# Reading moving operands and writing products in woven runs, in four gate products of a ConvFFN

## The chip, the cores and the metric

The kernel runs on one core of a Trainium2 chip. The metric is the device time of one execution in microseconds (us). The engines are named as the profile names them: PE is TensorE (PEld its weight loads), ACT is ScalarE, DVE is VectorE, POOL is GpSimd, and SP issues the transfers from HBM.

## The reference

The program computes a small decoder trunk in fp32 on 256 tokens of width 2048: one mLSTM layer, a gated ConvFFN, one layer of differential attention, a second ConvFFN and a last norm. The change lies in the first ConvFFN:

```python
def conv_ffn(xn, w_up, conv_w, conv_b, w_down):
    u = xn @ w_up                                  # (256, 2048) @ (2048, 2 * 5632)
    up = jnp.pad(u, ((0, 0), (CONV_W - 1, 0), (0, 0)))
    c = conv_b + up[:, 0:S] * conv_w[0]
    for j in range(1, CONV_W):
        c = c + up[:, j:j + S] * conv_w[j]
    gate, val = jnp.split(c, 2, axis=-1)
    return (jax.nn.silu(gate) * val) @ w_down
```

## The kernel before

Every fp32 number is split into two parts of type fp32r, a rounded high part and the low part that is left, and a product of two numbers is the sum of three products of parts (the one of both low parts is left out). TensorE multiplies a stationary operand of 128 x 128 with a moving operand of up to 512 columns and adds into a PSUM accumulator.

The up projections are computed by `gemm`. One call makes one *column pair*, 256 columns of the projection, from 16 k tiles of 128. Weights are stationary: each column half of a k tile (128 columns) is loaded once as its high part `wh` and once as its low part `wl`. Activations are the moving operand. For each k tile the high part `xh` (256 tokens) and the low part `xl` (256 tokens) lie side by side in one buffer, `xhl`. So per k tile and column half there are two matmuls on L411: `wh` against `xhl`, 512 columns into the whole accumulator, and `wl` against `xh`, 256 columns into its lower half. When the 16 k tiles are done, ScalarE copies the upper half of each of the two accumulators out (`low`, L417), VectorE adds it to the lower half (L418), and the caller's function takes the sum on.

Weights arrive by DMA as `raw`, 1 MB at a time; `granule` splits them four k tiles at a time: ScalarE writes the high parts (L376) and VectorE the low parts (L377) into one of five buffers `w2`. A call of `gemm` thus has four granules, k0 = 0, 4, 8 and 12, of 16 matmuls each.

`conv_ffn` goes through the projection in two parts of 11 pairs. For pair j of a part it calls `gemm` for the gate columns and then `gemm` for the value columns. Behind a gate call stand the convolution and a SiLU on ScalarE (L871), behind a value call the convolution and the product of gate and value (L881). A scheduler sets the order of all engines from the order in which the program is written, with small tasks put off by a number of granules (`later`, `tick`).

Of the kernel before, what the change touches and what calls it, by code (L numbers as in the profile page):

```python
# [19 lines left out]
P = 128  # L20
# [23 lines left out]
X_AT = (1, 2, 3, 5, 6, 8, 9)  # L44
SQ_AT = (6, 8, 10, 12)
CW = 256
WCOLS = 2048


# [19 lines left out]
def trunk(  # L69
# [22 lines left out]
    def tmp(name, rows=P, dt=F32):  # L92
        return work.tile([rows, T], dt, tag="tmp", name=name, bufs=8)
# [20 lines left out]
    def later(granules, fn):  # L114
        clock[1] += 1
        heapq.heappush(waiting, (clock[0] + granules, clock[1], fn))

    def tick():
        clock[0] += 1
        while waiting and waiting[0][0] <= clock[0]:  # L120
            heapq.heappop(waiting)[2]()
# [176 lines left out]
    def split(value, name):  # L298
        h, l, hl = block(F32R, name)
        act.activation(h, value, AF.Copy)  # L300
        dve.tensor_tensor(l, value, h.bitcast(F32), op=ALU.subtract)
        return h, l, hl
# [57 lines left out]
    def granule(w, c0, cw, k0, kn, raws, j, own=True):  # L360

        kc, hc = WCOLS // cw, WCOLS // cw // 2
        at, hc = k0 % kc, min(hc, kn - k0)
        if at == 0:
            raws[j] = wpool.tile([P, kc, cw], F32, tag="raw", name="raw", bufs=RAW)
            n = min(kc, kn - k0)
            loads.append(nc.sync.dma_start(raws[j][:, :n], w[k0 * P:(k0 + n) * P, c0:c0 + cw].rearrange("(k p) n -> p k n", p=P)))
        part = raws[j][:, at:at + hc]
        if not own:
            pairs = [block(F32R, "w2")[:2] for _ in range(hc)]  # L370
            for i, (h, l) in enumerate(pairs):
                act.activation(h, part[:, i], AF.Copy)
                dve.tensor_tensor(l, part[:, i], h.bitcast(F32), op=ALU.subtract)
            return pairs
        w2 = wpool.tile([P, WCOLS // cw // 2, 2, cw], F32R, tag="w2", name="w2", bufs=HL)
        act.activation(w2[:, :hc, 0], part, AF.Copy)  # L376
        dve.tensor_tensor(w2[:, :hc, 1], part, w2[:, :hc, 0].bitcast(F32), op=ALU.subtract)  # L377
        return [(w2[:, i, 0], w2[:, i, 1]) for i in range(hc)]

    def in_order(kn, hc, groups, lead, held=1):  # L380

        starts, groups = list(range(0, kn, hc)), list(groups)
        order = [(j, k) for j in groups[:lead] for k in starts[:-held]] + [(j, k) for j in groups[:lead] for k in starts[-held:]]
        return order + [(j, k) for j in groups[lead:] for k in starts], starts[-1]

    def gemm(xs, w, col0, pairs, evac, lead=1, narrow=()):

        kn = len(xs)
        order, last = in_order(kn, 4, pairs, lead)
        raws, accs = {}, {}
        for j, k0 in order:
            if k0 == 0:
                accs[j] = [acc_ps.tile([P, 2 * T], F32, tag="acc", name="acc") for _ in range(2)]
            ps = accs[j]
            halves = granule(w, col0 + j * CW, CW, k0, kn, raws, j)
            wide = j not in narrow
            for i, (wh, wl) in enumerate(halves):  # L400
                k = k0 + i
                xh, xl, xhl = xs[k]
                for n in range(2):
                    s = slice(n * P, (n + 1) * P)
                    one = ps[n][:, :T]
                    if wide:
                        ops = ((wh[:, s], xhl, ps[n]), (wl[:, s], xh, one))
                    else:
                        ops = ((wh[:, s], xh, one), (wh[:, s], xl, one), (wl[:, s], xh, one))
                    for o, (a, b, to) in enumerate(ops):  # L410
                        pe.matmul(to, a, b, start=(k == 0 and o == 0), stop=(k == kn - 1 and o == len(ops) - 1))  # L411
            if k0 == last:
                done = accs.pop(j)
                if wide:
                    for p in done:
                        low = tmp("low")
                        act.activation(low, p[:, T:], AF.Copy)  # L417
                        dve.tensor_tensor(p[:, :T], p[:, :T], low, op=ALU.add)  # L418
                evac(j, [p[:, :T] for p in done])
            tick()  # L420

    def gemm_tokens(xs, w, col0, groups, evac, cw=G, lead=1):

        kn, hc = len(xs), WCOLS // cw // 2
        order, last = in_order(kn, hc, groups, lead, held=4 // hc)
# [82 lines left out]
    def gemm_by_tokens(xs, w, col0, evac):  # L508
# [3 lines left out]
        for t in range(2):  # L512
            s = slice(t * P, (t + 1) * P)
            for k in range(kn):
                if t == 0 and k % 4 == 0:

                    halves += granule(w, col0, CW, k, kn, raws, 0, own=k < HL * 4)
                xh, xl, _ = xs[k]
# [8 lines left out]
    def mix(pair):  # L527

        (a11, a21), (a12, a22) = ((c[:, :P], c[:, P:]) for c in pair)
        s = block(F32, "sum")[2].rearrange("p (a n) -> p a n", a=4)  # L530
        dve.tensor_tensor(s[:, 0], a21, a22, op=ALU.add)
        dve.tensor_tensor(s[:, 1], s[:, 0], a11, op=ALU.subtract)
        dve.tensor_tensor(s[:, 2], a21, a11, op=ALU.subtract)
        dve.tensor_tensor(s[:, 3], a12, s[:, 1], op=ALU.subtract)
        h, l = (block(F32R, "mix")[2].rearrange("p (a n) -> p a n", a=4) for _ in range(2))
        act.activation(h, s, AF.Copy)
        dve.tensor_tensor(l, s, h.bitcast(F32), op=ALU.subtract)
        return [(h[:, i], l[:, i]) for i in range(4)]
# [42 lines left out]
    def residual(norm):  # L581
        def evac(g, ps, mix=None):
            if mix is not None:
                mixed_in(g, mix)
            for t in range(2):
                rows = stream[:, t, g * G:(g + 1) * G]
                dve.tensor_tensor(rows, ps[t], rows, op=ALU.add)
            if norm is not None:
                norm.add(g)
        return evac  # L590
# [87 lines left out]
    def mlstm(norm):  # L678
# [5 lines left out]
        def gates():  # L684
            gw = wpool.tile([P, WCOLS], F32, tag="raw", name="gw", bufs=RAW)[:, :KD * 16].rearrange("p (k n) -> p k n", n=16)

# [163 lines left out]
    def conv_ffn(layer, norm, evac_down, finish=None):  # L850

        cw = convs[layer]
        later(2, norm.rstd)
        half = FT // 2
        for part in range(2):
            hidden = [None] * half
            conv_of = {}

            def conv(ps, f):
                u = tmp("u")  # L860
                dve.tensor_tensor(u, ps, norm.r, op=ALU.mult)  # L861
                c = tmp("c")
                act.activation(c, u, AF.Identity, bias=cw[:, 3, f:f + 1], scale=cw[:, 2, f:f + 1])  # L863
                dve.scalar_tensor_tensor(c[:, 1:], u[:, :T - 1], cw[:, 1, f:f + 1], c[:, 1:], op0=ALU.mult, op1=ALU.add)
                dve.scalar_tensor_tensor(c[:, 2:], u[:, :T - 2], cw[:, 0, f:f + 1], c[:, 2:], op0=ALU.mult, op1=ALU.add)
                return c

            def evac_gate(j, ps):
                for n in range(2):
                    c = conv(ps[n], part * half + 2 * j + n)  # L870
                    act.activation(c, c, AF.Silu)  # L871
                    conv_of[2 * j + n] = c

            mixed = {}

            def evac_val(j, ps):
                pair = []
                for n in range(2):
                    f = 2 * j + n
                    c = conv(ps[n], FT + part * half + f)  # L880
                    dve.tensor_tensor(c, c, conv_of[f], op=ALU.mult)  # L881
                    hidden[f] = split(c, f"hid{f}")
                    pair.append(c)
                if 4 * (j // 2) in MIXED:
                    mixed[2 * j] = mix(pair)

            for j in range(half // 2):
                gemm(norm.sets[0], w_up[layer], part * half * P, [j], evac_gate)
                gemm(norm.sets[0], w_up[layer], D_FF + part * half * P, [j], evac_val)
            rows = w_down[layer, part * half * P:(part + 1) * half * P]  # L890
            if part == 0:
                gemm_sevenths(hidden, mixed, rows, 0, range(NG), residual(None), MIXED)
            elif finish is None:
                gemm_sevenths(hidden, mixed, rows, 0, range(NG), evac_down, MIXED)
            else:
                gemm_sevenths(hidden, mixed, rows, 0, range(NG - 1), evac_down, MIXED)
                finish(hidden, rows)
# [239 lines left out]
    def finish(hidden, rows):  # L1137
        gemm_tokens(hidden, rows[:, W0:], 0, [0], lambda j, ps: evac_last(NG - 1, ps), cw=T)
        gemm_by_tokens(hidden, rows, W1, tokens_done)

    conv_ffn(1, norm_f1, evac_last, finish=finish)


# [29 lines left out]
```

## Time and profile before

| What | Value |
|---|---|
| Three runs | 2247.5, 2247.64, 2247.94 us; median 2247.64 us |
| Profiled execution, span from the first to the last instruction | 2246.0 us |
| Mean granted TensorE clock | 0.999 |
| PE busy in the span | 2236.4 us |
| DVE, ACT, POOL busy | 1800.5, 1297.7, 112.4 us |
| Bytes read from HBM, rate over the span | 414.77 MB, 186 GB/s |

The page gives the span of the profiled execution and no other time of it; the runs are timed apart from it. Busy time is the time in which an engine had an instruction under way. Matmuls overlap their neighbours: the mean duration that a row gives for one is longer than its share of TensorE's time, which is read from a stretch of many matmuls divided by their count. Shapes stand as partitions x elements.

### The profile page before, as it was taken

How to read it: one execution, taken by the hardware profiler on the slowest of the kernel's cores; microseconds unless marked ns; L12 is line 12 of the kernel's file. 1: busy time of each engine (PE TensorE's matmuls, PEld its weight loads, DVE VectorE, ACT ScalarE, POOL GpSimd, SP SyncE). 2: the span in 40 equal slices, each digit the busy share in tenths (PEclk: the TensorE clock that was granted, in tenths of full speed). 3: DMA queues.
4: the chain of work that ended last, by engine and by line, in shares of the span. 5: the costliest groups of instructions: out<-in, count | busy, mean ns of one | idle time of the engine just before them, and what ended most of it. 6: DMA issues, size and time to landing. Idle time of an engine off the chain costs nothing.

```text
span 2246.0 us, 33469 instructions
## 1 busy us (share of the span) xinstructions
PE 2236.4 (100%) x12847; PEld 1953.4 (87%) x12847; DVE 1800.5 (80%) x3007; ACT 1297.7 (58%) x2011; POOL 112.4 (5%) x275
## 2 busy tenths in 40 slices
PE   9999999999999999999999999999999999999998
PEld 9888888888888888888888888888888888888888
DVE  6756868787788877879998985677877988778896
ACT  5455655665554565656655655556565555556554
POOL 0014000000000000000022102300000000000000
PEclk9999999999999999999999999999999999999999
DMA  8554546555545755546566555465555457555464
GB/s 278 177 176 149 186 162 211 192 188 188 187 160 188 234 188 188 190 148 206 193 204 196 161 173 162 154 202 187 188 188 188 159 188 245 190 189 189 145 216 150
DMA packets 325636, 419.04 MB, mean 187 GB/s; under 512 B 9102, under 2 KB 238820, under 8 KB 325476
## 3 DMA queue, kind: packets, MB, share of 16 engines
q1 hardware_dynamic: 325444, 416.89, 56.7%
q8 instruction: 101, 1.65, 0.3%
q14 instruction: 59, 0.48, 0.1%
q10 hardware_dynamic: 32, 0.01, 0.0%
HBM read 414.77 MB, written 2.10 MB: 186 GB/s over the span
## 4 chain that ended last, share of the span: by engine, by line
PE 99%; DVE 0%; ACT 0%; issue 0%; DVEq 0%
PE acc L411 54%; PE acc L503 16%; PE acc L437 14%; PE mix L493 6%; PE acc L493 4%; PE acc L656 2%; PE val_ps L335 1%; PE acc L521 1%; PE turn_ps L231 0%; PE as_ps L987 0%; PE warm_ps L130 0%; PE turn_ps L637 0%; PE hn_ps L357 0%; PE gps L695 0%; PE as_ps L988 0%; PE an_ps L357 0%
## 5 line engine op out<-in xcount | busy, mean ns | idle before, releaser
L377 DVE TENSOR_TENSOR w<-raw,w 128x1024 fp32r<-128x1024 f32 x679 | 826.6, 1222 | 269.6 <-ACT w L376 267.3
L376 ACT ACTIVATE w<-raw 128x1024 fp32r<-128x1024 f32 x679 | 714.0, 1058 | 490.8 <-PE acc L411 322.8
L411 PE MATMUL acc<-x_f,w 128*128 128x512 f32 (+1 forms) x5632 | 987.5, 337 | 0.0
L411 PEld LDWEIGHTS acc<-x_f,w 128*128 128x128 f32 x5632 | 861.5, 188 | 122.8
L503 PE MATMUL acc<-w,hid 128*128 128x512 f32 x1080 | 268.1, 394 | 0.0
L503 PEld LDWEIGHTS acc<-w,hid 128*128 128x128 f32 x1080 | 195.3, 188 | 39.0
L411 PE MATMUL acc<-x_at,w 128*128 128x512 f32 (+1 forms) x1024 | 182.1, 338 | 0.0
L411 PEld LDWEIGHTS acc<-x_at,w 128*128 128x128 f32 x1024 | 156.6, 188 | 21.9 <-issue 0.2
L458 ACT ACTIVATE w<-diff 128x1024 fp32r<-128x1024 f32 x89 | 94.1, 1057 | 113.1 <-DVE diff L451 83.2
L417 ACT ACTIVATE low<-acc 128x256 f32<-128x256 f32 x216 | 78.9, 385 | 130.6 <-PE acc L411 127.7
L459 DVE TENSOR_TENSOR w<-diff,w 128x1024 fp32r<-128x1024 f32 x89 | 108.9, 1223 | 39.5 <-ACT w L458 39.1
L437 PE MATMUL acc<-w,x_a 128*128 128x512 f32 x576 | 138.0, 396 | 0.0
L437 PEld LDWEIGHTS acc<-w,x_a 128*128 128x128 f32 x576 | 106.8, 188 | 24.2
L493 PE MATMUL mix<-w,mix 128*128 128x256 f32 x801 | 119.4, 281 | 0.0
L418 DVE TENSOR_TENSOR acc<-acc,low 128x256 f32<-128x256 f32 x216 | 84.3, 430 | 38.4 <-ACT low L417 38.0
L493 PEld LDWEIGHTS mix<-w,mix 128*128 128x128 f32 x801 | 107.1, 188 | 2.4 <-DVE w L459 0.2
L863 ACT ACTIVATE c<-u,conv 128x256 f32<-128x256 f32 x176 | 98.2, 593 | 5.9 <-DVE u L861 5.6
L458 ACT ACTIVATE w<-raw 128x768 fp32r<-128x768 f32 x89 | 74.7, 840 | 36.7 <-PE acc L503 22.8
L968 POOL TENSOR_TENSOR sw<-sw,sin_t 32x256 f32<-32x256 f32 x32 | 39.1, 1235 | 1076.9 <-DVE sw L967 1026.4
L437 PE MATMUL acc<-w,x_at 128*128 128x512 f32 x384 | 91.4, 395 | 0.0
L459 DVE TENSOR_TENSOR w<-raw,w 128x768 fp32r<-128x768 f32 x89 | 84.9, 953 | 2.5 <-ACT w L458 2.3
L493 PE MATMUL acc<-w,hid 128*128 128x256 f32 x450 | 86.3, 281 | 0.0
(318 smaller groups left out, 2343.8 us busy)
## 6 DMA issues: line engine op xcount, KB each, us to landing
raw<-in_w_up_dram SPq DMA_DIRECT2D x176, 1024.0 KB
raw<-in_w_down_dram SPq DMA_DIRECT2D x79, 1024.0 KB
raw<-in_m_w_in_dram SPq DMA_DIRECT2D x46, 1024.0 KB
raw<-in_w_kv_dram SPq DMA_DIRECT2D x32, 1024.0 KB
raw<-in_m_w_out_dram SPq DMA_DIRECT2D x16, 1024.0 KB
raw<-in_w_q_dram SPq DMA_DIRECT2D x16, 1024.0 KB
raw<-in_w_o_dram SPq DMA_DIRECT2D x16, 1024.0 KB
raw<-in_w_down_dram SPq DMA_DIRECT2D x15, 512.0 KB
```

The lines of the kernel that those rows point to most:

```text
L376: act.activation(w2[:, :hc, 0], part, AF.Copy)
L377: dve.tensor_tensor(w2[:, :hc, 1], part, w2[:, :hc, 0].bitcast(F32), op=ALU.subtract)
L411: pe.matmul(to, a, b, start=(k == 0 and o == 0), stop=(k == kn - 1 and o == len(ops) - 1))
L417: act.activation(low, p[:, T:], AF.Copy)
L418: dve.tensor_tensor(p[:, :T], p[:, :T], low, op=ALU.add)
L437: pe.matmul(ps[t], a[:, s], b, start=(k == 0 and o == 0), stop=(k == kn - 1 and o == 2))
L458: act.activation(w2[:, :m, 0], src, AF.Copy)
L459: dve.tensor_tensor(w2[:, :m, 1], src, w2[:, :m, 0].bitcast(F32), op=ALU.subtract)
L493: pe.matmul(to, u, v, start=start and o == 0, stop=end and o == 2 and to is not a and to is not b, skip_group_check=True)
L503: pe.matmul(ps, u[:, s], v, start=(k0 + i == 0 and o == 0), stop=(k0 + i == kn - 1 and o == 2), skip_group_check=True)
L656: pe.matmul(ps[j], a, b, start=(k == 0 and o == 0 and j % 2 == 0), stop=(k == KD - 1 and o == 2), skip_group_check=True)
L863: act.activation(c, u, AF.Identity, bias=cw[:, 3, f:f + 1], scale=cw[:, 2, f:f + 1])
```

## The change

Before a matmul is issued in `gemm`, its moving operand and its output may be *woven*. `woven(ap, streams, run)` cuts the columns into `streams` equal stretches and walks through them by turns, `run` columns of the first, `run` of the second and so on, then the next `run` of each. Both operand and output are walked in the same way, so that each column's product lands where it did. The table `WEAVES` names four calls, all of layer 0 and of the gate columns: pairs 4 and 6 of part 0 and pairs 4 and 6 of part 1. It gives one (streams, run) for each of a call's four granules; (1, 1) leaves a granule as it was, which two of the sixteen are. With two streams a matmul of 512 columns takes turns between `xh` and `xl`.

```diff
+WEAVES = {(0, 0, 4): ((1, 1), (2, 2), (2, 4), (2, 8)), (0, 0, 6): ((2, 16), (2, 32), (2, 64), (4, 2)),
+          (0, 1, 4): ((2, 2), (1, 1), (2, 8), (2, 4)), (0, 1, 6): ((4, 2), (4, 8), (2, 16), (8, 2))}
...
+    def woven(ap, streams, run):
+        if streams == 1:
+            return ap
+        return ap.rearrange("p (s a r) -> p a s r", s=streams, r=run)
+
-    def gemm(xs, w, col0, pairs, evac, lead=1, narrow=()):
+    def gemm(xs, w, col0, pairs, evac, lead=1, narrow=(), weaves=((1, 1),)):
...
                     for o, (a, b, to) in enumerate(ops):
+                        b, to = (woven(v, *weaves[k0 // 4 % len(weaves)]) for v in (b, to))
                         pe.matmul(to, a, b, start=(k == 0 and o == 0), stop=(k == kn - 1 and o == len(ops) - 1))
...
-                gemm(norm.sets[0], w_up[layer], part * half * P, [j], evac_gate)
+                gemm(norm.sets[0], w_up[layer], part * half * P, [j], evac_gate, weaves=WEAVES.get((layer, part, j), ((1, 1),)))
```

On TensorE, the gate call of pair 4 in part 0, at the border of its first granule (left plain) and its second (two streams, runs of two). `acc` are the two accumulators, `x_f0_3` and so on the k tiles of the activations, `w2` the split weights; the last column is the shape of the output. Before:

```order
L411 MATMUL acc_4815<-x_f0_3_3337,w2_4819 128x512
L411 MATMUL acc_4815<-x_f0_3_3337,w2_4819 128x256
L411 MATMUL acc_4816<-x_f0_3_3337,w2_4819 128x512
L411 MATMUL acc_4816<-x_f0_3_3337,w2_4819 128x256
L411 MATMUL acc_4815<-x_f0_4_3538,w2_4838 128x512
L411 MATMUL acc_4815<-x_f0_4_3538,w2_4838 128x256
L411 MATMUL acc_4816<-x_f0_4_3538,w2_4838 128x512
L411 MATMUL acc_4816<-x_f0_4_3538,w2_4838 128x256
```

And with the change:

```order
L421 MATMUL acc_4815<-x_f0_3_3337,w2_4819 128x512
L421 MATMUL acc_4815<-x_f0_3_3337,w2_4819 128x256
L421 MATMUL acc_4816<-x_f0_3_3337,w2_4819 128x512
L421 MATMUL acc_4816<-x_f0_3_3337,w2_4819 128x256
L421 MATMUL acc_4815<-x_f0_4_3538,w2_4838 128x128x2x2
L421 MATMUL acc_4815<-x_f0_4_3538,w2_4838 128x64x2x2
L421 MATMUL acc_4816<-x_f0_4_3538,w2_4838 128x128x2x2
L421 MATMUL acc_4816<-x_f0_4_3538,w2_4838 128x64x2x2
```

Nothing moved; the line is L421 instead of L411, and the output of 512 columns is now 128 turns of two streams with two columns each.

On TensorE, the gate call of pair 6 in part 1, at the border of its third granule (two streams, runs of 16) and its fourth (eight streams, runs of two). Before:

```order
L411 MATMUL acc_8642<-x_f0_11_3748,w2_8686 128x256
L411 MATMUL acc_8643<-x_f0_11_3748,w2_8686 128x512
L411 MATMUL acc_8643<-x_f0_11_3748,w2_8686 128x256
L411 MATMUL acc_8642<-x_f0_12_3935,w2_8705 128x512
L411 MATMUL acc_8642<-x_f0_12_3935,w2_8705 128x256
L411 MATMUL acc_8643<-x_f0_12_3935,w2_8705 128x512
L411 MATMUL acc_8643<-x_f0_12_3935,w2_8705 128x256
```

And with the change:

```order
L421 MATMUL acc_8642<-x_f0_11_3748,w2_8686 128x8x2x16
L421 MATMUL acc_8643<-x_f0_11_3748,w2_8686 128x16x2x16
L421 MATMUL acc_8643<-x_f0_11_3748,w2_8686 128x8x2x16
L421 MATMUL acc_8642<-x_f0_12_3935,w2_8705 128x32x8x2
L421 MATMUL acc_8642<-x_f0_12_3935,w2_8705 128x16x8x2
L421 MATMUL acc_8643<-x_f0_12_3935,w2_8705 128x32x8x2
L421 MATMUL acc_8643<-x_f0_12_3935,w2_8705 128x16x8x2
```

Here too only the shapes differ. VectorE, ScalarE, GpSimd and SP have the same rows before and after but for line numbers.

## The prediction

> **What bounds the kernel now.** I read the head of the page first, then the chain of waits, then the four stretches that the change touches.
>
> ```profile
> span 2246.0 us, 33469 instructions
> PE 2236.4 (100%) x12847; PEld 1953.4 (87%) x12847; DVE 1800.5 (80%) x3007; ACT 1297.7 (58%) x2011; POOL 112.4 (5%) x275
> PEclk9999999999999999999999999999999999999999
> ...
> PE 99%; DVE 0%; ACT 0%; issue 0%; DVEq 0%
> ```
>
> TensorE is busy for 2236.4 of 2246.0 us at the full granted clock, and the chain that ended last is 99% TensorE. The idle remainder, 9.6 us, is all the slack there is, and none of it lies in the stretches below. A microsecond added to a matmul should therefore come out as a microsecond of the program, and one taken away likewise, until another engine becomes late.
>
> The four changed calls of `gemm` are the gate calls of pair 4 and pair 6 in both halves of the first ConvFFN. A call ends where ScalarE copies the upper half of its two accumulators (L417), and a SiLU behind that copy (L871) tells a gate call from a value call. That puts the four calls here, in the view of stretches (length, then busy time of each engine, granted clock, DMA share, GB/s):
>
> ```profile
> core 0: us, PE busy (x) PEld busy (x) DVE busy (x) ACT busy (x) POOL busy (x), PEclk, DMA share, GB/s
> 483.69:494.95 11.26, 11.26 (x66) 9.81 (x65) 10.10 (x21) 6.99 (x11) 0.00 (x0) 1.00 0.60 188
> 528.49:539.75 11.26, 11.26 (x66) 9.81 (x65) 9.08 (x16) 6.46 (x10) 0.00 (x0) 1.00 0.57 188
> 846.47:857.73 11.26, 11.26 (x66) 9.80 (x65) 10.11 (x21) 6.98 (x11) 0.00 (x0) 1.00 0.56 187
> 891.27:902.53 11.26, 11.26 (x66) 9.80 (x65) 9.08 (x16) 6.46 (x10) 0.00 (x0) 1.00 0.59 186
> ```
>
> TensorE fills all of each, at clock 1.00. VectorE, the next, is busy for 10.1 us at most. Who waits for whom there says the same (engine and line waited for, total us, times, longest; from 480 to 545 us):
>
> ```profile
> ACT w L376 <- PE acc L411: 18.2, 17, 1.8
> DVE w L377 <- ACT w L376: 11.3, 12, 1.6
> ACT low L417 <- PE acc L411: 7.8, 6, 1.4
> ```
>
> ScalarE waits for TensorE to give a weight buffer back, and VectorE waits for ScalarE. The weights are ready early and TensorE alone sets the pace.
>
> Its pace is read from the chain's long pieces (start, us, line, count), and for the changed line from the starts of the copies behind three calls in a row:
>
> ```profile
> 28.87 5.68 PE acc L656 x48
> 291.19 18.87 PE acc L437 x81
> 409.64 231.17 PE acc L411 x1321
> ```
>
> ```profile
> 483.69 0.74 ACT L417 ACTIVATE low<-acc 128x256 f32<-128x256 f32 x2 [1.39 <-PE acc L411]
> 494.95 0.74 ACT L417 ACTIVATE low<-acc 128x256 f32<-128x256 f32 x2 [0.87 <-PE acc L411]
> 506.09 0.74 ACT L417 ACTIVATE low<-acc 128x256 f32<-128x256 f32 x2 [1.39 <-PE acc L411]
> ```
>
> L656 holds matmuls of 256 columns only: 5.68 / 48 = 118.3 ns each. L437 holds 512 only: 18.87 / 81 = 233.0 ns. So a column costs (233.0 - 118.3) / 256 = 0.448 ns, and a start 118.3 - 256 x 0.448 = 3.6 ns. L411 issues one of each in turn: 231.17 / 1321 = 175.0 ns on average. Two calls take 506.09 - 483.69 = 22.40 us, which for 128 matmuls is again 175.0. TensorE spends its time on columns streamed, hardly on starts.
>
> **The change, part by part.** The order of every engine is the same before and after, tile by tile; no instruction, semaphore wait or DMA is added, removed or moved. Only the shape of some matmuls on L411 differs. A granule (four k tiles, two column halves) has 8 matmuls of 512 columns and 8 of 256, 8 x 768 = 6144 columns. Of the 16 granules in the four calls two are left plain, so 14 are woven: 224 matmuls, 14 x 6144 = 86,016 columns, 224 x 175.0 ns = 39.2 us of TensorE time. That is 1.7% of the span, and all that this change can touch. By run length:
>
> - runs of 2 columns: 5 granules, 30,720 columns, 15,360 runs;
> - runs of 4: 2 granules, 3,072 runs; runs of 8: 3 granules, 2,304 runs;
> - runs of 16: 2 granules, 768 runs; of 32: 192 runs; of 64: 96 runs.
>
> Together 21,792 runs. The product is the same, the same column goes to the same place in the accumulator; only the order in which TensorE walks through them changes, on the reading and on the writing side alike.
>
> What does such a walk cost? No matmul of before has a moving operand or an output in runs, so the price is bounded by the nearest rows.
>
> *Lower end.* A woven matmul streams as many columns as a plain one, so all that it could save beside them is its start of 3.6 ns: 224 x 3.6 ns = 0.8 us. I see no reason for that either, but it gives the lower end, -0.8 us.
>
> *Upper end.* If each run were priced like the start of a matmul, 21,792 x 3.6 ns = 78 us. Between these stand two rows of other engines that show what jumps do and what a slower walk through the same memories costs:
>
> ```profile
> L376 ACT ACTIVATE w<-raw 128x1024 fp32r<-128x1024 f32 x678 | 713.5, 1059 | 490.8 <-PE acc L411 322.8 <-PE acc L437 62.5 <-PE acc L503 45.9
> L458 ACT ACTIVATE w<-raw 128x768 fp32r<-128x768 f32 x89 | 74.7, 840 | 36.7 <-PE acc L503 22.8 <-PE acc L493 5.2 <-ACT c L863 2.9
> L536 ACT ACTIVATE mix<-sum 128x512 fp32r<-128x512 f32 x26 | 16.1, 618 | 1.1 <-DVE sum L534 1.1
> L300 ACT ACTIVATE hid<-c 128x256 fp32r<-128x256 f32 x88 | 31.8, 402 | 1.6 <-DVE c L881 1.6
> L954 ACT ACTIVATE qh<-aq 128x256 fp32r<-128x256 f32 x8 | 3.4, 422 | 0.0
> ```
>
> ScalarE on L376 writes 1024 columns as four runs of 256 with gaps between; L536 and L300 write 512 and 256 in one run. The unbroken pair gives (618 - 402) / 256 = 0.844 ns a column, hence 618 + 512 x 0.844 = 1050 ns for 1024. Measured are 1059: three jumps for 9 ns. L954's qh, read as two runs of 128, takes 422 against 402, 20 ns for one jump. So jumps cost little or nothing beside a column stream where runs are long, but no row has a run below 128 columns. For a slower walk, ScalarE's pace is (1059 - 840) / 256 = 0.855 ns a column, 0.407 more than TensorE's. All 86,016 columns at that pace would add 35.0 us; the runs of two columns alone, 30,720 x 0.407 = 12.5 us.
>
> *The value I take* is zero. What a jump does on L376 is far closer to nothing than to a change of pace, and the TensorE rows say that it streams at one price per column whether 256 or 512 are asked for, with 3.6 ns for everything else about an instruction. Runs of two are the ones this is least safe for: they hold 70% of the runs (15,360 / 21,792).
>
> [...]
>
> *Cover and what follows.* Nothing is hidden by luck: a slower woven matmul would go straight into the end, since TensorE has no idle time in the four stretches. What comes later would be late by the same amount and nothing else: behind a woven matmul stand only further matmuls, then the copy on L417; ScalarE and VectorE already wait for TensorE, so a delay lengthens their waits and frees the weight buffers, and with them SP's next weight DMA, later by as much. Weight loads would still be hidden: 9.8 us of loads against 11.26 us of matmuls.
>
> The sum: the profiled span 2246.0 + 0 = 2246.0 us. The median of the runs is 2247.64, so 1.64 us lie around the span, which the change does not touch: 2247.6 us. I count a difference under 0.2% (4.5 us) as no change, about what a measurement of this kernel can tell.
>
> **The rivals.**
>
> 1. *Runs of two pay, longer ones don't.* From some run length down TensorE can't fetch or place columns in time and falls to about ScalarE's pace. For it: two columns are far below the 128 of the shortest run in the trace. Against: nothing but the low cost of jumps on L376. +12.5 us: 2260.1 us. It decides from 11,100 columns at that pace (4.5 us / 0.407 ns), that is from two granules of 6144.
>
> 2. *Every run pays one column's time.* A jump empties one slot of the stream. For it: 20 ns for one jump on L954. Against: 9 ns for three on L376. 21,792 x 0.448 ns = 9.8 us: 2257.4 us.
>
> 3. *Every woven column pays, whatever the run.* An access that is not contiguous leaves the fast path as a whole. +35.0 us: 2282.6 us. For it: that TensorE's price per column, half of ScalarE's, may rest on unbroken streams, as all its matmuls in the trace are unbroken. Against: the copies on L376 show no such path on ScalarE, as their four runs cost what one run would. [...]
>
> 4. *The change does not do what it says*, the walk being merged back into one run. The order shows shapes such as 128x128x2x2 for the changed matmuls, which can't be merged since the two streams lie 256 columns apart. If it were so, the time would be that of the forecast; I give it no chance of its own.
>
> **How the numbers follow.** Forecast, no cost: 0.66. Rival 1: 0.10. Rival 2: 0.08. Rival 3: 0.12. Dearer still, up to the 78 us of a start for every run: 0.02. Faster by over 4.5 us has no mechanism, as 0.8 us is the most that I can find: 0.02. So faster 0.02, within 0.2% 0.66, slower 0.10 + 0.08 + 0.12 + 0.02 = 0.32. The forecast's own range is 2246.6 to 2249. The range that is to hold 8 in 10 must take in rivals 1 and 2: up to 2262, which leaves out rival 3 and beyond, 0.14, and the 0.02 below 2246.
>
> **What would show it.** By shape, the matmuls of the changed line: forms such as 128x128x2x2 and 128x64x2x2 with the mean of the plain forms, which are now
>
> ```profile
> L411 PE MATMUL acc<-x_f,w 128*128 128x512 f32 x2816 | 984.8, 394 | 0.0
> L411 PE MATMUL acc<-x_f,w 128*128 128x256 f32 x2816 | 787.3, 280 | 0.0
> ```
>
> that is 394 and 280 ns, and copies on L417's successor still 11.26 us after the value call's. Rival 1 shows as calls of unequal length: pair 4's gate in the first half with one granule of runs of two would grow by 2.5 us (6144 x 0.407), pair 6's gate in the second half, with two, by 5.0. By rival 2 these two would grow by 2.4 us (3072 + 1536 + 768 = 5376 runs) and 3.3 us (3072 + 768 + 384 + 3072 = 7296 runs). Rival 3 gives 7.5 us (three woven granules) and 10.0 us (four). If the span grows and no call's length does, my reading of the bound is wrong, and not the price.

## The result, and the profile after

The kernel with the change takes 2259.39 us (median of runs from 2259.11 to 2259.66), the kernel before 2247.79 us beside it: 11.6 us more, a ratio of 1.0051 with a 95% interval of 1.0037 to 1.0065. The forecast was 2247.6 us with a range of 2246.0 to 2262.0. The range held the time, but the forecast itself, no difference, was wrong.

The head of the page of the changed kernel:

```profile
span 2257.9 us, 33469 instructions
PE 2248.1 (100%) x12847; PEld 1958.7 (87%) x12847; DVE 1800.6 (80%) x3007; ACT 1297.3 (57%) x2011; POOL 112.0 (5%) x275
PEclk9999999999999999999999999999999999999999
...
PE 99%; DVE 0%; ACT 0%; issue 0%; DVEq 0%
```

The span grew by 11.9 us and TensorE's busy time by 11.7. VectorE's, ScalarE's and GpSimd's busy times are what they were to within 0.4 us, and so is the clock (0.999). The bound was read rightly; the matmuls themselves became dearer. By shape, in a view that does not tell woven matmuls from plain ones:

```profile
L421 PE MATMUL acc<-x_f,w 128*128 128x512 f32 x2816 | 995.6, 397 | 0.0
L421 PE MATMUL acc<-x_f,w 128*128 128x256 f32 x2816 | 793.0, 282 | 0.0
```

Before, 984.8 and 787.3 us stood here. How much each weave costs shows when the calls are cut at the granules, from the start of a granule's first matmul to the start of the next granule's first. The view of stretches of the changed kernel; in order they are the plain granule of the first gate call, then (streams, run) = (2, 2), (2, 4), (2, 8) of that call, (4, 2) of the second, and (4, 2), (4, 8), (8, 2) of the fourth:

```profile
core 0: us, PE busy (x) PEld busy (x) DVE busy (x) ACT busy (x) POOL busy (x), PEclk, DMA share, GB/s
483.66:486.46 2.80, 2.80 (x18) 2.45 (x17) 2.54 (x6) 2.51 (x5) 0.00 (x0) 1.00 0.63 210
486.46:490.45 3.99, 3.99 (x18) 2.91 (x17) 3.91 (x10) 1.07 (x1) 0.00 (x0) 1.00 0.38 120
490.45:493.50 3.05, 3.05 (x19) 2.56 (x17) 1.74 (x4) 1.68 (x3) 0.00 (x0) 1.00 0.97 329
493.50:496.44 2.94, 2.94 (x19) 2.51 (x17) 2.16 (x5) 1.69 (x3) 0.00 (x0) 1.00 0.06 16
538.56:543.93 5.37, 5.37 (x18) 3.31 (x17) 1.67 (x3) 1.44 (x2) 0.00 (x0) 1.00 0.59 185
897.16:902.51 5.35, 5.35 (x18) 3.30 (x17) 4.14 (x9) 2.51 (x5) 0.00 (x0) 1.00 0.60 196
902.51:905.36 2.85, 2.85 (x18) 2.48 (x18) 1.52 (x3) 1.06 (x1) 0.00 (x0) 1.00 0.00 0
908.24:914.04 5.80, 5.80 (x18) 3.32 (x17) 1.60 (x4) 1.47 (x2) 0.00 (x0) 1.00 0.57 183
```

A plain granule takes 2.80 us. The five with runs of two take 3.99, 4.07, 5.37, 5.35 and 5.80 us, together 10.6 us too much. The nine others are between 0.0 and 0.25 us too long, together 1.0. The sum is the whole of the 11.6 us. Two things are new in it: a run of two is far dearer in four or eight streams (5.35 to 5.80 us a granule) than in two (3.99 and 4.07), and the price is gone, nearly, at runs of four (3.05 in two streams).

### The profile page after: what moved, and what is told of

It reads as the page before. It is cut to its first block, busy times and chain, and to the rows that moved or that the text cites. A ratio compares the mean times of both kernels' runs of the same rounds, so it can differ in the third digit from the quotient of the medians.

```text
span 2257.9 us, 33469 instructions
## 1 busy us (share of the span) xinstructions
PE 2248.1 (100%) x12847; PEld 1958.7 (87%) x12847; DVE 1800.6 (80%) x3007; ACT 1297.3 (57%) x2011; POOL 112.0 (5%) x275
## 4 chain that ended last, share of the span: by engine, by line
PE 99%; DVE 0%; ACT 0%; issue 0%; DVEq 0%
PE acc L421 54%; PE acc L513 16%; PE acc L447 14%; PE mix L503 6%; PE acc L503 4%; PE acc L666 2%; PE val_ps L337 1%; PE acc L531 1%; PE turn_ps L233 0%; PE as_ps L997 0%; PE warm_ps L132 0%; PE turn_ps L647 0%; PE hn_ps L359 0%; PE gps L705 0%; PE as_ps L998 0%; PE an_ps L359 0%
## 5 line engine op out<-in xcount | busy, mean ns | idle before, releaser
L378 ACT ACTIVATE w<-raw 128x1024 fp32r<-128x1024 f32 x679 | 714.1, 1058 | 498.4 <-PE acc L421 330.0
L421 PE MATMUL acc<-x_f,w 128*128 128x512 f32 (+1 forms) x5632 | 999.1, 340 | 0.0
L421 PEld LDWEIGHTS acc<-x_f,w 128*128 128x128 f32 x5632 | 866.3, 188 | 129.6 <-issue 6.1
L421 PE MATMUL acc<-x_at,w 128*128 128x512 f32 (+1 forms) x1024 | 182.1, 338 | 0.0
L421 PEld LDWEIGHTS acc<-x_at,w 128*128 128x128 f32 x1024 | 156.8, 188 | 21.8 <-issue 0.2
L468 ACT ACTIVATE w<-diff 128x1024 fp32r<-128x1024 f32 x89 | 94.1, 1057 | 112.2 <-DVE diff L461 82.4
```

The costliest lines, as they stand in the source:

```text
L468: act.activation(w2[:, :m, 0], src, AF.Copy)
```

## The experiments

**Which runs pay.** Two kernels with a smaller table:

```diff
 (without the runs of two)
+WEAVES = {(0, 0, 4): ((1, 1), (1, 1), (2, 4), (2, 8)), (0, 0, 6): ((2, 16), (2, 32), (2, 64), (1, 1)),
+          (0, 1, 4): ((1, 1), (1, 1), (2, 8), (2, 4)), (0, 1, 6): ((1, 1), (4, 8), (2, 16), (1, 1))}
 (with them alone)
+WEAVES = {(0, 0, 4): ((1, 1), (2, 2), (1, 1), (1, 1)), (0, 0, 6): ((1, 1), (1, 1), (1, 1), (4, 2)),
+          (0, 1, 4): ((2, 2), (1, 1), (1, 1), (1, 1)), (0, 1, 6): ((4, 2), (1, 1), (1, 1), (8, 2))}
```

> The change with its five granules of runs of two columns left plain; the nine woven in runs of 4 to 64 stay. Theory 1 (runs of two carry nearly all): by the matmul starts in the changed kernel's profile what is left costs 0.9 us: 2248.7 us, no difference that can be told from before by much. Theory 2 (every run pays alike): 6,432 of 21,792 runs stay, of 11.6 us that is 3.4: 2251.2 us. Theory 3 (every woven column pays alike): nine of 14 granules stay, 7.5 us: 2255.3 us.

> The change with only its five granules of runs of two columns; the other nine are plain. Theory 1: 10.6 us of the 11.6 stay: 2258.4 us. Theory 2: 15,360 of 21,792 runs, 8.2 us: 2256.0 us. Theory 3: five of 14 granules, 4.1 us: 2251.9 us. If two streams cost less per run than four and eight, as the starts say (0.4 ns against 0.8 and 1.0), the gate calls of pair 6 in the second half of the projection grow by more than twice as much as those of pair 4: from 11.26 to about 16.5 us against about 12.5.

Measured: without the runs of two 2248.77 us (ratio 1.0004 to the kernel before, interval 0.9995 to 1.0012), with them alone 2258.66 us (1.0048, 1.0033 to 1.0064). Theory 1 gave 2248.7 and 2258.4. Theory 3 gave 2255.3 and 2251.9, both outside the intervals. Theory 2 gave 2251.2, outside its interval (a ratio of 1.0015), and 2256.0, which lies inside its own (1.0036); it is out by the first, and by the granules above, where the same 3,072 runs of two cost 1.2 us in two streams and 3.0 in eight. The gate call of pair 6 in the second half went from 11.26 to 16.47 us in the second kernel, that of pair 4 there to 12.53. These are the intervals between the copies behind the calls, as in the prediction:

```profile
850.30 0.74 ACT L427 ACTIVATE low<-acc 128x256 f32<-128x256 f32 x2 [1.39 <-PE acc L421]
862.83 0.74 ACT L427 ACTIVATE low<-acc 128x256 f32<-128x256 f32 x2 [0.87 <-PE acc L421]
...
896.37 0.74 ACT L427 ACTIVATE low<-acc 128x256 f32<-128x256 f32 x2 [1.39 <-PE acc L421]
912.84 0.39 ACT L427 ACTIVATE low<-acc 128x256 f32<-128x256 f32 x1 [3.98 <-PE acc L421]
```

**Reading or writing.** The change weaves both. A sweep gives 38 of the 44 calls of each ConvFFN a weave of their own, on both sides or on one:

```diff
-                        b, to = (woven(v, *weaves[k0 // 4 % len(weaves)]) for v in (b, to))
+                        streams, run, side = weave
+                        if side != "write":
+                            b = woven(b, streams, run)
+                        if side != "read":
+                            to = woven(to, streams, run)
```

> In both ConvFFNs every gate and value call of the up projections has one weave for all its four granules, 38 of 44 calls, in the first layer in one order and in the second in the reverse. In a third of them operand and output are woven, in a third the operand alone (read), in a third the output alone (write). With one side alone the products land in other columns than they should, so the values are not the reference's; counts, shapes and order of the instructions are. A plain call takes 11.2 us. From the matmul starts of the changed kernel's profile, calls woven on both sides should take: two streams, runs of 2: 16.0 us; of 4: 12.1; of 8: 11.7; of 16: 11.5; four streams, runs of 2: 21.4; of 8: 11.3; eight streams, runs of 2: 23.2. Theory R (the reading side has to fetch its lines again): the read calls take as long as those woven on both sides, the write calls 11.2. Theory W (the accumulator pays): the write calls take as long, the read calls 11.2. Theory S (each side pays a part and the parts add): both are longer than 11.2, and their excesses sum to that of both sides. Theory M (the slower side decides): both alone are as long as both together. R, W and S give a program of about 2247.8 + 2 x 2 x 42 = 2416 us, M about 2500.

The stretches of eight calls, from first matmul to first matmul: plain; (2, 2) on both sides, read, write; (4, 2) on both sides, read, write; and two streams with runs of one, which was only run on the read side:

```profile
416.76:427.96 11.20, 11.20 (x66) 9.78 (x65) 9.96 (x19) 8.40 (x14) 0.00 (x0) 1.00 0.59 189
427.96:444.05 16.09, 16.09 (x66) 11.64 (x65) 7.86 (x13) 6.72 (x11) 0.00 (x0) 1.00 0.43 133
605.83:621.86 16.03, 16.03 (x66) 11.62 (x65) 8.57 (x13) 6.80 (x11) 0.00 (x0) 1.00 0.43 136
922.45:933.66 11.21, 11.21 (x67) 9.79 (x66) 8.41 (x13) 6.58 (x11) 0.00 (x0) 1.00 0.59 189
479.46:500.91 21.45, 21.45 (x66) 13.28 (x65) 8.44 (x14) 6.82 (x11) 0.00 (x0) 1.00 0.39 121
657.28:678.73 21.45, 21.45 (x67) 13.27 (x65) 7.86 (x13) 6.80 (x11) 0.00 (x0) 1.00 0.36 117
967.26:978.46 11.20, 11.20 (x67) 9.79 (x66) 7.74 (x12) 6.78 (x11) 0.00 (x0) 1.00 0.60 189
1056.86:1067.34 10.48, 10.48 (x67) 9.63 (x66) 7.74 (x12) 6.74 (x11) 0.00 (x0) 1.00 0.64 203
```

Theory R's times hold: reading alone costs as much as both (16.03 and 21.45 us against 16.09 and 21.45), writing alone nothing (11.21 and 11.20 against 11.20). The reason it gives, lines fetched again, no run shows. All twelve write weaves, down to runs of two in sixteen streams, are within 0.02 us of plain. The program took 2425 us in its one run, against 2416 expected. By the starts of the matmuls, reading costs this much (median ns from a matmul of 512 columns to the next; plain 233; runs of one in 8 and 16 streams are from the next run):

| Run | 2 streams | 4 streams | 8 streams | 16 streams |
|---|---|---|---|---|
| 1 | 218 | 280 | 488 | 435 |
| 2 | 332 | 445 | 486 | 447 |
| 4 | 252 | 268 | 275 | 243 |
| 8 | 243 | 235 | 239 to 249 | - |
| 16 | 240 | - | - | - |

The last row of the stretches was a surprise: two streams with runs of *one* column are not slower than plain but 6% faster, 10.48 us a call.

The change itself, its own table on one side, was timed too:

> The change with its table as it is, on the written side alone: outputs woven, operands read plain. The products land in other columns than they should, so the values are not the reference's. Theory R (the whole price lies on the reading side, as the sweep's calls say): 2247.8 us, the time of before. If the two sides hinder each other only in a mix of granules as here, some of the 11.6 us stays.

> The change with its table as it is, on the read side alone: operands woven, outputs plain; values not the reference's for the same reason. Theory R: the whole excess, 2259.4 us. If writing took a share: less than that, by what the written side alone costs.

Measured: written side alone 2248.15 us (ratio 1.0000, 0.9991 to 1.0009), read side alone 2259.78 us (1.0052, 1.0039 to 1.0066). That settles the side.

**What in the reading.** All outputs plain, and the operand read in 38 walks; the read view of `gemm` becomes two columns by turns (`d`), every q-th column (`st`), runs of r with gaps (`sr`), or plain or in streams from an offset (`w`; the buffer is four columns longer, to leave room for it):

```diff
+        if kind == "d":
+            return v.rearrange("p (b s a) -> p b a s", s=2, a=form[1])
+        if kind == "st":
+            return v.rearrange("p (a q) -> p q a", q=form[1])
+        if kind == "sr":
+            return v.rearrange("p (a q r) -> p q a r", q=form[1], r=form[2])
...
+        v = x[:, at:at + width]
+        return v if streams == 1 else v.rearrange("p (s a r) -> p a s r", s=streams, r=run)
```

> All writes plain; the moving operand of each gate and value call of the up projections is read in one of 38 walks over the same buffer. The products land in other columns than they should, so the values are not the reference's. Known from the sweep: a plain call takes 11.2 us, two streams with runs of one 10.5, of two 16.0, four streams with runs of one 13.5, of two 21.5. Theory P (pairs): columns are fetched in twos, the first and the second by separate readers; a reader that finds its next column among the same four neighbours pays little, one that needs a new four at each step pays double. Then two columns by turns from places 4 to 128 apart: 10.5 us at every distance; 2 apart: 11.2. Every second column: 21.5, though nothing jumps; every fourth and beyond: 21.5 or more. Runs of two at every fourth column: 21.5; runs of four with gaps: 11.2 to 12.3. Plain from an offset of 1, 2 or 3 columns: 11.2; runs of four in two streams from an offset of two: about 16, as each run lies across two fours. Theory T (turns): the turn of the address generator's inner loop costs. Then every second, fourth or further column: 11.2; runs of two at every fourth column: at least 16; runs of four 12.3 whatever the gap; an offset changes nothing: 12.2. Theory L (lines): two reads in a row from the same four columns are enough. Then every second column 11.2, every fourth 21 or more, runs of two 11.2; the sweep already speaks against it.

Eight calls: two columns by turns, 4 apart; 2 apart; every second column; runs of two at every fourth column; runs of four at every eighth; two streams with runs of four from offset 0; plain from offset 1; two streams with runs of four from offset 2:

```profile
479.83:490.31 10.48, 10.48 (x66) 9.63 (x65) 9.90 (x21) 6.89 (x12) 0.00 (x0) 1.00 0.62 202
490.31:501.50 11.19, 11.19 (x66) 9.78 (x65) 8.54 (x13) 6.63 (x11) 0.00 (x0) 1.00 0.57 187
501.50:523.33 21.83, 21.83 (x67) 13.27 (x65) 9.16 (x16) 6.69 (x11) 0.00 (x0) 1.00 0.36 121
629.96:651.78 21.82, 21.82 (x66) 13.26 (x65) 10.69 (x21) 7.00 (x11) 0.00 (x0) 1.00 0.30 98
717.11:728.35 11.24, 11.24 (x66) 9.80 (x65) 10.97 (x19) 6.20 (x10) 0.00 (x0) 1.00 0.14 52
1007.46:1019.61 12.15, 12.15 (x65) 10.20 (x65) 7.82 (x12) 6.61 (x11) 0.00 (x0) 1.00 0.51 170
1030.88:1042.31 11.43, 11.43 (x67) 9.92 (x65) 7.75 (x12) 6.78 (x11) 0.00 (x0) 1.00 0.57 185
1101.61:1117.64 16.03, 16.03 (x66) 11.74 (x65) 7.90 (x12) 6.60 (x11) 0.00 (x0) 1.00 0.40 132
```

The sixth is the sweep's two streams again. For the others theory P gave 10.5, 11.2, 21.5, 21.5, 11.2 to 12.3, 11.2 and about 16, and fits these seven to within 0.4 us. Not every one of the 38 fits so well: every 8th, 16th and 32nd column took 20.8 to 21.0 us where 21.5 or more was given, and runs of four with gaps of twelve columns 10.9 where 11.2 or more was. Every second column, a walk with a single jump, takes nearly double (21.83 us against 11.20): theories T and L both had 11.2 there. Turns 4, 8, 16, 32, 64 and 128 columns apart are all at 10.5. The same runs of four are 12.15 us where each lies in one aligned four and 16.03 where it lies across two. Set against these walks, the times go with what every *other* column of the walk does: where the first, third, fifth column and so on, and likewise the second, fourth, sixth, find their next one in the same aligned four for a step or more, a call above takes 10.48 to 12.15 us; where each time they need a new four, 16.03 to 21.83, up to nearly double the plain 11.2.

For runs of two theory L had 11.2 us a call, as much as plain, since two reads in a row fall into the same four; they took 15.8 to 23.1 us. The aligned runs of four above took 11.24 and 12.15 us, and two columns by turns, 4 apart, 10.48.

**Why streams count.** Left over was that runs of two cost half as much in two streams as in four. Only the 256-column matmuls are read in a walk here, in both ConvFFNs (the expectation speaks of the first alone):

```diff
+        if form == "two, no return":
+            return x.rearrange("p (s a q r) -> p q a s r", s=2, q=2, r=2)[:, 0]
+        if form == "two, return":
+            return x.rearrange("p (s b a r) -> p b a s r", s=2, b=2, r=2)[:, 0]
...
```

> Only the 256-column matmuls of the first up projection have their operand read in a walk (128-column streams of the 512-column buffer; values not the reference's); all else is plain. Plain they start 118 ns apart from the next. The question is why runs of two cost 50 ns in two streams and 107 in four. Theory M (memory): each of the two readers keeps about two fours of columns, so that with two streams the second run of a four finds it still there; with four streams it doesn't. Then two streams of twos that skip every other two, so that no four is visited twice: 225 ns; two streams that return: 168; four streams of ones at every second column, two visits to a four, two fours by turns for each reader: 168; at every column, four visits: 141; four streams of twos: 225; two streams of ones at every second column: 118 or less. Theory N (number of streams): what counts is how many streams the address generator turns through: two streams 168 whether they return or not, four 225.

The calls of two streams of twos without return, with return, two streams of ones at every second column, four streams of ones at every second column, and at every column:

```profile
828.49:843.85 15.36, 15.36 (x66) 12.73 (x65) 7.82 (x12) 6.69 (x11) 0.00 (x0) 1.00 0.44 139
843.85:856.68 12.83, 12.83 (x65) 11.45 (x64) 9.24 (x16) 6.39 (x11) 0.00 (x0) 1.00 0.48 162
856.68:867.89 11.21, 11.21 (x66) 9.81 (x65) 7.79 (x12) 6.76 (x11) 0.00 (x0) 1.00 0.62 189
867.89:880.70 12.81, 12.81 (x67) 11.45 (x65) 10.67 (x21) 7.00 (x12) 0.00 (x0) 1.00 0.52 164
880.70:892.55 11.85, 11.85 (x66) 10.46 (x65) 8.16 (x12) 6.57 (x11) 0.00 (x0) 1.00 0.55 178
```

By their starts the 256-column matmuls take 227, 160, 117, 161 and 136 ns, and 235 in four streams of twos that return; theory M gave 225, 168, at most 118, 168, 141 and 225. Theory N wanted the first two alike at 168. Two streams are cheaper where the second run of a four comes two runs after the first (160 ns); where it doesn't come, two streams (227 ns) cost nearly as much as four (235). That each of two readers keeps about two fours, as theory M has it, is the author's estimate; no run shows such readers. (From the plain 512-column matmuls to the walked ones behind them it takes up to about 25 ns longer too, which is in the calls' lengths.)

**A version that beats both.** Runs of one in two streams read faster than plain (10.48 us a call against 11.20), and of the two sides only the reading showed in the times. The next kernel stores the activations of both up projections so that this walk gives the tokens in order:

```diff
...
+        if name.startswith("x_f"):
+            ps = ps.rearrange("p (a s) -> p s a", s=2)
+            hv, lv = (v.rearrange("p (s a) -> p s a", s=2) for v in (h, l))
+            act.activation(hv, ps, AF.Identity, scale=scale)
...
+                        if paired:
+                            b = b.rearrange("p (h s a) -> p h a s", s=2, a=P)
                         pe.matmul(to, a, b, start=(k == 0 and o == 0), stop=(k == kn - 1 and o == len(ops) - 1))
```

> The kernel before, with the activations of both up projections stored with the even tokens of a part in its first 128 columns and the odd ones in its last 128, and read by turns from the two, so that the tokens come out in their order; outputs are written plain. All 88 calls are read as two streams with runs of one. By the sweep a call takes 10.5 us in place of 11.2, 88 x 0.7 = 62 us: 2186 us. Rival: at that pace the weights come late, since VectorE is busy for 9.1 to 10.1 us of a call; if the calls stay at 10.9 on average the time is 2221 us. Rival: the distance of 128 columns is not as good as the 256 that the 512-column matmuls had in the sweep, and nothing is won: 2248 us.

2185.32 us, ratio 0.9722 (0.9709 to 0.9735); expected were 2186. Span and TensorE, by which the whole gain is TensorE's:

```profile
span 2183.5 us, 33469 instructions
PE 2173.9 (100%) x12847; PEld 1939.7 (89%) x12847; DVE 1793.6 (82%) x3007; ACT 1296.2 (59%) x2011; POOL 112.5 (5%) x275
...
L419 PE MATMUL acc<-x_f,w 128*128 128x512 f32 x2816 | 922.5, 382 | 0.0
L419 PE MATMUL acc<-x_f,w 128*128 128x256 f32 x2816 | 766.3, 273 | 0.0
```

394 and 280 ns became 382 and 273, and TensorE's busy time fell by 62.5 us, as the span did. ScalarE and VectorE now read every second column of PSUM to store the activations, and take no longer for it: 466 and 478 ns on average, 466 and 479 before. The next kernel does the same for all other moving operands that could be stored so, weights included:

```diff
+    def by_turns(v):
+        return v.rearrange("p (c s a) -> p c a s", s=2, a=P)
...
+            part, hi, lo = halved(part, True), halved(hi, False), halved(lo, False)
         act.activation(hi, part, AF.Copy)
...
-                        pe.matmul(ps[t], a[:, s], b, start=(k == 0 and o == 0), stop=(k == kn - 1 and o == 2))
+                        pe.matmul(ps[t], a[:, s], by_turns(b), start=(k == 0 and o == 0), stop=(k == kn - 1 and o == 2))
```

> The kernel that reads the up projections' activations by turns, with the same done for the query projection's activations and for all weights that are moving operands (the products by tokens and the down projections): ScalarE and VectorE store them with even columns in the first half of each 256 and odd ones in the second, TensorE reads the halves by turns, outputs are plain. By the sweep a matmul of 512 columns gains 14.5 ns, one of 256 8.5: 2,832 x 14.5 + 2,133 x 8.5 ns + 8 calls x 0.7 us = 41 + 18 + 6 = 65 us, from 2185.3 to 2120 us. Rival: ScalarE and VectorE read every second column of the weights now and pay for it as TensorE does, double per split; then VectorE, 80% busy before, becomes the bound and the time is above 2247.8.

2193.75 us (0.976, 0.9746 to 0.9773), 8 us slower than the kernel above and not the 65 us faster that were expected. The splits of the weights are a large part of why:

```profile
PE 2138.1 (98%) x12847; PEld 1934.5 (88%) x12847; DVE 1865.6 (85%) x3007; ACT 1436.2 (66%) x2011; POOL 119.8 (5%) x275
...
L400 DVE TENSOR_TENSOR w<-raw,w 128x1024 fp32r<-128x1024 f32 x678 | 876.0, 1299 | 188.2 <-ACT w L399 186.0
L399 ACT ACTIVATE w<-raw 128x1024 fp32r<-128x1024 f32 x678 | 807.1, 1207 | 327.8 <-PE acc L436 262.3 <-PE acc L462 23.8 <-PE acc L530 8.1
L485 ACT ACTIVATE w<-diff 128x1024 fp32r<-128x1024 f32 x89 | 128.3, 1442 | 129.3 <-DVE diff L476 125.0 <-PE acc L530 4.0
```

TensorE's busy time shrank by 35.8 us to 2138.1, but it now stands idle for 54 of the 2192.0 us of the span, where it was 9.6. Waits for splits are 25 us of that; another 10 us are two waits of the sequence layers (mLSTM and attention), at L363 for ScalarE's L354 (5.5 us) and at L341 (4.8 us, with no releaser in the profile). The rows of L399 and L400 mix two kinds of splits, as weights that are stationary operands are still read plain. Told apart by their read patterns in the trace, the 236 splits of L399 that read every second column take 1472 ns on average (1122 to 1820) and were 1058 before, those of L400 1438 and were 1222. In the seven products (products made of seven smaller ones, of blocks of weights and of their differences, `diff`) ScalarE's went from 1057 to 1442 ns and VectorE's from 1223 to 1386. That is 13 to 39% more; not double, as the rival had it, but enough to be late there. So the seven products were left plain again (the down projections and parts of three other products):

```diff
-                    for i, (wh, wl) in enumerate(granule(w, col0 + g * G, G, k0, kn, raws, g, turns=True)):
+                    for i, (wh, wl) in enumerate(granule(w, col0 + g * G, G, k0, kn, raws, g)):
...
-                                pe.matmul(ps, u[:, s], by_turns(v), start=(k0 + i == 0 and o == 0), stop=(k0 + i == kn - 1 and o == 2), skip_group_check=True)
+                                pe.matmul(ps, u[:, s], v, start=(k0 + i == 0 and o == 0), stop=(k0 + i == kn - 1 and o == 2), skip_group_check=True)
```

> The kernel that reads the up projections' activations by turns, with the same for the query projection's activations and for the weights of the products by tokens; the down projections with their seven products, where VectorE was nearly full and the weights came late in the run before, are as they were. Gain by the sweep: 1,248 matmuls of 512 columns x 14.5 ns + 264 of 256 x 8.5 ns + 8 calls x 0.7 us = 18 + 2 + 6 = 26 us, if ScalarE's and VectorE's slower splits stay hidden behind TensorE: 2185.3 - 26 = 2159 us. Rival: weights come late in these stages too, and the time is 2185 or more.

2173.14 us, ratio 0.967 (0.9657 to 0.9683): the best of all, 12 of the 26 us expected over the kernel with the up projections alone. TensorE's busy time fell by 23 us, from 2173.9 to 2150.9, but its idle time rose from 9.6 to 20.4 us. Of these 11 us 9.6 are the two waits named above, at L363 for ScalarE's L354 (5.3 us) and at L341 (4.3 us), which the kernel with the up projections alone does not have; why they came up stays open.

## Why the prediction was wrong

*The bound* was right: TensorE alone, no slack in the four stretches, each microsecond of a matmul one of the program. TensorE's busy time grew by 11.7, the span by 11.9.

*The counts* were right: 14 granules, 86,016 columns, five granules of runs of two.

*The value taken, zero, was the step that failed.* The sum had no term for runs of two, and the five granules of them cost 10.6 us (the nine others 1.0). Zero was chosen because three jumps cost ScalarE 9 ns on L376 and TensorE has one price per column whether 256 or 512 are asked for. Neither row could tell. L376's runs are 256 columns long and tell nothing of runs of two; and that plain streams have a constant price of 0.448 ns does not say that this is the price of a column. Nor is it the least that a column can cost, since runs of one in two streams go at 0.427 ns (218.5 / 512). I had named runs of two as the ones least safe, with 70% of the runs, and still gave the sum no term for them.

*Rival 1 was what happened*: runs of two pay, longer ones hardly. Forecast were 12.5 us for the 30,720 columns, measured 10.6 in the granules and 10.7 between the timed kernels (2258.66 - 2247.93). The size was near by luck, as its price was ScalarE's pace for each column alike, while it really differs by streams: 1.2 to 1.3 us too long per granule in two, 2.6 in four, 3.0 in eight. In the call of pair 4 it gave 2.5 us where 1.2 were measured for that granule, in the call of pair 6 5.0 where it was 5.55. Its turning point lies between runs of two and of four columns (3.99 and 3.05 us a granule in two streams, 2.80 plain).

*Rival 2*, 0.448 ns a run, has a time near the measured one (2257.4) but is wrong. Without the runs of two 6,432 of the 21,792 runs remain, 2.9 us by that price; 0.8 us were measured, with an interval of the ratio that includes none and ends just below 2.9 us. The lengths of the calls are clearer. From first matmul to first matmul, pair 4's in the first half took 12.78 us (the first four stretches above) and pair 6's in the second half 16.88, which is 1.6 and 5.7 more than a plain 11.2; this rival gave 2.4 and 3.3. Most of the 20 ns on L954 that spoke for it seem to be that line's own, as its unbroken 512 columns, `kh`, take 632 ns (median) against the 618 of L536.

*Rival 3* is wrong: granules in runs of 4 to 64 were to cost 2.5 us each and cost 0.25 or less. On the written side alone not even runs of two cost anything (2248.15 us, ratio 1.0000); runs of one were not run there.

*The lower end*, -0.8 us with no mechanism for a gain, holds for this table, but the reason was wrong: I took columns streamed as a fixed price, and an order of reading that beats the plain one exists (218 ns for 512 columns against 233).

## What to carry to other kernels

An fp32 moving operand was read best where the odd and the even columns of the walk each stay in an aligned four for several steps in a row: two contiguous streams taken by turns, one column each, 4 to 256 columns apart, gave 6% over a plain read (10.48 us a call against 11.20). Storing the operand for it cost nothing where ScalarE and VectorE read it from PSUM (466 and 478 ns, 466 and 479 before), but 13 to 39% per split where they read weights from SBUF (1386 ns against 1223 to 1472 against 1058), so do it where they have room. Runs of two, and strides of two or more in one stream, were dear to read here (15.8 to 23.1 us a call, 1.4 to 2.1 times the plain 11.2); aligned runs of four took at most 275 ns for 512 columns where plain took 233; how the output is woven in runs of two or more did not matter (within 0.02 us a call). When a bound on a cost comes from rows in another range of sizes, as runs of 128 did for runs of two, give the unknown its own term rather than zero.

## What was unexpected of the hardware

- A plain contiguous fp32 read is not the fastest: 233 ns for 512 columns against 218, 118 against 109 for 256, at clock 1.00 in both.
- Where the aligned fours lie shows in the times: plain reads from an offset of 1, 2 and 3 columns took 237, 233 and 230 ns, yet runs of four in two streams went from 252 ns to 331 when shifted by two.
- The two readers of theory P, and that each keeps about two fours, were the author's estimate from the times of walks; no run shows them. Times that they don't give: runs of four with gaps of twelve columns took 226 ns, less than the plain 233; every 8th column (432) cost less than every second (452); runs of two in sixteen streams cost less (447) than in eight (486); runs of eight were dearer in two streams (243) than in four (235).
